# One pair more of the first MLP products in VectorE's written order

## The chip, the cores and the metric

The kernel runs on one core of one Trainium2 chip. Its time is the device time of one launch in microseconds (us); three runs of the kernel before gave 1718.39, 1720.16 and 1721.22 us, and the median, 1720.16, is the time before. Engines are called PE (TensorE), DVE (VectorE), ACT (ScalarE), POOL (GpSimd) and SP (SyncE, which issues most of the DMAs here).

## The reference

Two sequences of 512 tokens with 1024 features go through a trunk of two layers in float32: a Fourier token mixer and an MLP, then grouped-query attention and an MLP, each behind an RMS norm and with a residual, and a last RMS norm. The change lies in the MLPs alone:

```python
def sq_relu_mlp(h, w_up, w_down):
    a = jnp.maximum(h @ w_up, 0)
    return (a * a) @ w_down
...
        x = x + sq_relu_mlp(rms_norm(x, mlp_norm[i]), mlp_w_up[i], mlp_w_down[i])
```

with `w_up` of 1024 x 4096 and `w_down` of 4096 x 1024, the same weights for both sequences.

## The kernel before

**Numbers and products.** Every float32 matrix is split into two float32r halves: ACT casts it to the high half (line 82) and DVE subtracts that from the original to get the low half (line 83). A product of two split matrices is three matmuls per block. The MLP's first product, `h @ w_up`, is done by a 2x2 scheme with seven block products in place of eight (as Strassen and Winograd do it). The two sequences are the two columns of the scheme, the two halves of the features its inner index, and two neighbouring blocks of 128 hidden units its rows. Such two blocks are a pair. Layer 0 has 16 pairs; layer 1 has 14 and four hidden blocks done plainly.

**One pair.** A pair p takes seven products of 12 matmuls each (4 feature blocks x 3 matmuls of 128 x 512, line 833). `Pair.first` and `Pair.second` multiply the row of raw weights (a11, a12) with the operands b11 and b21; they fill the PSUM bank `self.o`. `Pair.rest` does the other five, with sums of weight blocks as the left factor: s2 into bank ob, s3 into oc, s1 into od, then a22 added on to oc and s4 added on to od. Behind each of them DVE adds a finished bank to something kept: line 911 (the first addition, ob + t gives u2), line 915 (the second, oc + u2 gives u3), line 924 (the third, od + u3), line 933 (oc + u2, after a22's product) and line 942 (od + u2, after s4's product). The matmuls that add on to oc or od may start only when line 915 or line 924 has read that bank. ACT then squares the results (lines 848, 849), POOL takes four differences of them (lines 950 to 953), and ACT's and SP's DMA queues write seven results to memory (line 843; those issued by SP are the spills called t1 to t4).

**What is prepared meanwhile.** While pair p is multiplied, DVE and ACT prepare pair p + 1: its sums of weight blocks (`sums_13`, lines 882 and 883, and `sum_2`, line 886, and `sum_4`, line 894) and the splits of these and of its row. `split_row` splits the row of raw weights, 128 x 1024, for `first` and `second`; `split_23` splits s2 and s3 together, `split_1` splits s1 and a22, `split_4` splits s4. The raw weights of pair p + 2 are loaded by SP (line 91) into a pool of five buffers, which hold two loads and one tile of sums for each pair.

**Order.** The tables `AHEADS = (8, 6)` say for how many pairs of each layer `first` and `second` are done ahead, in a first sweep over the pairs (the value is `ah` in the code). For these pairs only the five products of `rest` are left in the second sweep; the row of pair `ah` and of every later one is split, and its two products done, in the second sweep (such a pair is `late`). The framework's scheduler sets the order of each engine's instructions from the order of the program and its own planning; inside `tc.manual_schedule(engines={ET.DVE})` DVE's instructions stay in the order in which the code writes them. In the second sweep that holds for the pairs p < ah; later pairs are left to the scheduler. Each engine works off its list strictly in order, and so does SP with its DMA issues.

Of the kernel before, what the change touches and what calls it, by code (L numbers as in the profile page):

```python
# [40 lines left out]
def trunk_kernel(ctx, tc, x_in, xt_in, y_out, dcos, dsin, feat, rope, gfour, gcol, grow, gfin,  # L41
# [22 lines left out]
    def tm(shape=(P, 512), dt=F32):  # L64
        return tmp.tile(list(shape), dt, tag="t2", name=nm("t"))
# [4 lines left out]
    def ps():  # L70
        return psp.tile([P, 512], F32, tag="ps", name=nm("ps"))
# [569 lines left out]
    ET = mybir.EngineType  # L641
# [185 lines left out]
    def product(o, w, h, first=True):  # L827

        n = len(h)
        for k in range(n):  # L830
            sl = slice(k * P, (k + 1) * P)
            for i, (x, y) in enumerate(((0, 0), (0, 1), (1, 0))):
                nc.tensor.matmul(o, w[x][:, sl], h[k][y], start=first and k + i == 0,  # L833
                                 stop=k == n - 1 and i == 2, skip_group_check=not first)

    def first_product(l, blocks, rows, ahead):
        def b(name):
            return [(h[0][:, i], h[1][:, i]) for h in blocks.b[name] for i in range(2)]
# [6 lines left out]
        np_, ah = NPS[l], AHEADS[l]  # L845

        def squares(t, src):
            nc.scalar.activation(t, src, AF.Relu)
            nc.scalar.activation(t, t, AF.Square)  # L849

        class Pair:
# [55 lines left out]
            def rest(self, nxt, fill=iter(())):  # L907
                ob, oc, od = ps(), ps(), ps()
                u2, u3, t = tm(), tm(), self.t
                product(ob, self.s2, b("t2"))  # L910
                nc.vector.tensor_add(u2, ob, t[:, 0])  # L911
                if nxt:
                    nxt.sums_13()
                product(oc, self.s3, b("t3"))
                nc.vector.tensor_add(u3, oc, u2)
                if self.late:
                    self.second()
                if nxt:
                    nxt.sum_2()
                if nxt and self.late:  # L920
                    nxt.split_row()
                next(fill, None)
                product(od, self.s1, b("t1"))
                nc.vector.tensor_add(u3, od, u3)  # L924
                if nxt and nxt.p == ah:
                    nxt.split_row()
                squares(u3, u3)
                if nxt:
                    nxt.split_23()
                product(oc, self.a22, b("t4"), False)  # L930
                next(fill, None)
                v = tm()
                nc.vector.tensor_add(v, oc, u2)
                squares(v, v)
                if nxt:
                    nxt.sum_4()
                    nxt.split_1()
                next(fill, None)
                if nxt:
                    nxt.split_4()  # L940
                product(od, self.s4, b("b22"), False)
                nc.vector.tensor_add(t[:, 0], od, u2)
                squares(t[:, 0], t[:, 0])
                return t[:, 1], t[:, 0], v, u3
# [91 lines left out]
        def early(ahead):  # L1036

            pairs[-1].first()
            pairs[-1].second()
            pairs[-1].late = False  # L1040
            for _ in range(3):
                yield next(ahead)

        for p, pair in enumerate(pairs[:-1]):
            if p >= ah:
                pair.first()
            with tc.manual_schedule(engines={ET.DVE}) if p < ah else nullcontext():
                done = pair.rest(pairs[p + 1], early(ahead) if not last and p == np_ - 2 else iter(()))
            if p + 2 < len(pairs):
                if p + 2 >= ah:  # L1050
                    pairs[p + 2].load()
                pairs[p + 2].load_sums()
            elif last:
                last[0].load()
            if not last and p == np_ - 3:
                next(ahead)
            pair.out(*done, queue=nc.sync if last or p < np_ - 2 else nc.gpsimd)
# [12 lines left out]
    def second_product(l, blocks, rows, late=lambda: None, ready=lambda m: None):  # L1070
# [179 lines left out]
        def finish(m):  # L1250
            left[m] -= 1
            if left[m] == 0:
                nc.vector.tensor_add(xs[0, m][:, 1], xs[0, m][:, 1], e[m])
                nc.vector.tensor_add(xs[1, m], xs[1, m], e[m].unsqueeze(1).broadcast_to([P, 2, 512]))
                ready(m)

        first_product(l, blocks, rows, ahead)
        e += [tm() for _ in range(4)]
        items, waiting = [], []
# [296 lines left out]
    for n in range(1, len(heads) + 1):  # L1556
        pts, nxt = [], []
# [309 lines left out]
```

## Time and profile before

| | us |
|---|---|
| time of the three runs, median | 1720.16 |
| time of the profiled execution | 1717.6 |
| its span, first to last instruction | 1715.8 |
| PE busy in the span | 1691.0 |
| DVE busy | 1239.0 |
| ACT busy | 857.8 |
| POOL busy | 335.5 |

Rows of the timeline give the start, the duration, the engine, the line, the operation, output and input tiles, how many instructions were merged into the row and, in brackets, how long the engine had stood idle before it and whose work ended that idle time. Matmuls overlap, so that a row of twelve lasts a little longer than the distance from its start to the next row's start; distances between starts give the pace. Letters ahead of an arrow name what is written, those behind it what is read: ps is a PSUM bank, w and u are tiles of halves or results, t a smaller temporary, raw a tile of raw weights or of their sums.

In layer 0 the second sweep's pair 8 (`ah`) begins with PE at 257.9 us, in layer 1 pair 6 at 1213.5 us.

### The profile page before, as it was taken

To read this page: it belongs to the slowest core of one execution; us is meant where nothing else is said; L and a number is where in the kernel's file an instruction comes from. 1 tells how busy PE (TensorE), PEld (TensorE's weight loads), DVE (VectorE), ACT (ScalarE), POOL (GpSimd) and SP (SyncE) were. 2 spreads that over 40 slices of the span, in tenths; PEclk is the share of its full clock that TensorE was granted. 3 is DMA by queue.
4 is the path that set the end of the run, shared out by engine and by line. 5 is a ranking of instruction groups with operands and counts; after the bars stand their busy time and mean duration, and the time that the engine had idled before them with its cause. 6 is when DMAs were issued, how large, how long until landed. Compare 5 with 4: busy or idle time off the path is not lost. (4 is left out here: it accounts for less than half of the span.)

```text
span 1715.8 us, 21892 instructions
## 1 busy us (share of the span) xinstructions
PE 1691.0 (99%) x7847; PEld 1395.8 (81%) x7847; DVE 1239.0 (72%) x1836; ACT 857.8 (50%) x1508; POOL 335.5 (20%) x302
## 2 busy tenths in 40 slices
PE   9999999999999999999999999999999999999997
PEld 6988887888788888888877888788788888888886
DVE  8679776456887879976588834687655479787865
ACT  6666445446343434457687714554444544344334
POOL 1321442321000000232244303114422200000004
PEclk9999999999999999999999999999999999999999
DMA  9742554449554645610000213335534686455322
GB/s 322 191 143 95 196 202 163 161 172 367 197 197 138 214 148 175 232 42 28 26 25 1 99 50 123 110 114 197 181 142 148 225 303 237 163 204 193 115 74 99
DMA packets 103679, 266.33 MB, mean 155 GB/s; under 512 B 10177, under 2 KB 10177, under 8 KB 103570
## 3 DMA queue, kind: packets, MB, share of 16 engines
q1 hardware_dynamic: 87410, 232.95, 38.4%
q10 hardware_dynamic: 14112, 25.70, 4.0%
q0 software_dynamic: 2048, 6.29, 1.8%
q8 instruction: 61, 1.00, 0.2%
q14 instruction: 48, 0.39, 0.1%
HBM read 189.93 MB, written 73.92 MB: 154 GB/s over the span
## 5 line engine op out<-in xcount | busy, mean ns | idle before, releaser
L833 PE MATMUL ps<-u,w 128*128 128x512 f32 x4656 | 1068.9, 390 | 5.3 <-DVE w L83 1.2
L833 PEld LDWEIGHTS ps<-u,w 128*128 128x128 f32 x4656 | 873.4, 188 | 192.3 <-DVE w L83 2.7
L82 ACT CAST w<-raw 128x1024 fp32r<-128x1024 f32 (+1 forms) x224 | 217.6, 981 | 435.8 <-PE ps L833 266.6
L83 DVE TENSOR_TENSOR w<-raw,w 128x1024 fp32r<-128x1024 f32 (+1 forms) x224 | 258.0, 1154 | 71.9 <-ACT w L82 71.5
L159 POOL TENSOR_TENSOR t<-t,t 128x512 f32<-128x512 f32 (+1 forms) x56 | 79.0, 1410 | 738.1 <-ACT t L157 682.0
L83 DVE TENSOR_TENSOR u<-u,u 128x1024 fp32r<-128x1024 f32 x132 | 157.6, 1220 | 25.8 <-ACT u L82 25.2
L82 ACT CAST u<-u 128x1024 fp32r<-128x1024 f32 x132 | 132.4, 1044 | 70.5 <-PE ps L833 48.5
L77 PE MATMUL ps<-u,u 128*128 128x512 f32 (+2 forms) x388 | 150.0, 388 | 1.9 <-DVE u L496 1.4
L1089 DVE TENSOR_TENSOR u<-ps,u 128x512 f32<-128x512 f32 x160 | 109.4, 686 | 53.9 <-PE ps L833 53.3
L78 PE MATMUL ps<-u,u 128*128 128x512 f32 (+2 forms) x388 | 144.8, 373 | 1.4 <-DVE u L83 1.4
L79 PE MATMUL ps<-u,u 128*128 128x512 f32 (+2 forms) x388 | 144.5, 372 | 0.0
L833 PE MATMUL ps<-u,u 128*128 128x512 f32 x576 | 138.2, 391 | 2.4 <-DVE t L924 2.3
L833 PEld LDWEIGHTS ps<-u,u 128*128 128x128 f32 x576 | 107.6, 188 | 27.1 <-DVE t L924 2.6
L950 POOL TENSOR_TENSOR u<-u 128x512 f32<-128x512 f32 x28 | 36.6, 1305 | 411.3 <-ACT u L849 411.3
L83 DVE TENSOR_TENSOR u<-ps,u 128x512 fp32r<-128x512 f32 (+4 forms) x118 | 74.6, 650 | 17.4 <-ACT u L82 16.2
L78 PEld LDWEIGHTS ps<-u,u 128*128 128x128 f32 x388 | 73.4, 189 | 14.1 <-DVE u L83 3.9
L77 PEld LDWEIGHTS ps<-u,u 128*128 128x128 f32 x388 | 73.5, 190 | 13.8 <-DVE u L496 1.6
L79 PEld LDWEIGHTS ps<-u,u 128*128 128x128 f32 x388 | 73.1, 188 | 13.0 <-DVE u L83 0.4
L911 DVE TENSOR_TENSOR t<-ps,u 128x512 f32<-128x512 f32 x30 | 20.7, 690 | 81.8 <-PE ps L833 63.8
L82 ACT CAST u<-ps 128x512 fp32r<-128x512 f32 (+4 forms) x118 | 64.6, 562 | 28.8 <-PE ps L79 10.9
L816 DVE TENSOR_TENSOR u<-ps,u 128x512 f32<-128x512 f32 (+1 forms) x48 | 30.8, 644 | 64.8 <-PE ps L79 64.8
L77 PE MATMUL ps<-u,w 128*128 128x512 f32 (+2 forms) x192 | 64.9, 338 | 0.0
(237 smaller groups left out, 2005.8 us busy)
## 6 DMA issues: line engine op xcount, KB each, us to landing
raw<-w_up SPq DMA_DIRECT2D x82, 512.0 KB, 4.5
u<-spill_t SPq DMA_DIRECT2D x60, 512.0 KB, 6.1
raw<-w_sum SPq DMA_DIRECT2D x56, 512.0 KB, 4.0
u<-spill_b SPq DMA_DIRECT2D x45, 512.0 KB, 5.2
spill_t<-u SPq DMA_DIRECT2D x87, 256.0 KB, 2.0
spill_b<-t ACTq DMA_DIRECT2D x60, 256.0 KB, 3.2
raw<-w_row SPq DMA_DIRECT2D x28, 512.0 KB, 4.1
park<-u SPq DMA_DIRECT2D x24, 512.0 KB, 3.3
```

The costliest lines, as they stand in the source:

```text
L77: nc.tensor.matmul(out, lh, rh, start=first, stop=False)
L78: nc.tensor.matmul(out, lh, rl, start=False, stop=False)
L79: nc.tensor.matmul(out, ll, rh, start=False, stop=last)
L82: nc.scalar.copy(dst_hi, src)
L83: eng.tensor_sub(dst_lo, src, f32(dst_hi))
L159: nc.gpsimd.tensor_add(acc[q][:, :n], acc[q][:, :n], s[:, :n])
L816: nc.vector.tensor_add(x[:, :n], o[:, :n], x[:, :n])
L833: nc.tensor.matmul(o, w[x][:, sl], h[k][y], start=first and k + i == 0, stop=k == n - 1 and i == 2, skip_group_check=not first)
L911: nc.vector.tensor_add(u2, ob, t[:, 0])
L950: eng.tensor_sub(t[:, 0], b12, b11)
L1089: nc.vector.tensor_add(x, o, x)
```

## The change

The written order of DVE holds for p <= ah, that is for one pair more in each layer: pair 8 in layer 0 and pair 6 in layer 1. Within the code of that pair, the call that splits the next pair's row is moved from ahead of the third product (s1) to behind the third addition, line 924, where pair ah - 1 already had it. Pairs after `ah` keep it where it was. Products, tiles and instructions are the same in number and kind.

```diff
@@ -917,12 +917,12 @@
                     self.second()
                 if nxt:
                     nxt.sum_2()
-                if nxt and self.late:
+                if nxt and self.p > ah:
                     nxt.split_row()
                 next(fill, None)
                 product(od, self.s1, b("t1"))
                 nc.vector.tensor_add(u3, od, u3)
-                if nxt and nxt.p == ah:
+                if nxt and ah - 1 <= self.p <= ah:
                     nxt.split_row()
                 squares(u3, u3)
                 if nxt:
@@ -1044,7 +1044,7 @@
         for p, pair in enumerate(pairs[:-1]):
             if p >= ah:
                 pair.first()
-            with tc.manual_schedule(engines={ET.DVE}) if p < ah else nullcontext():
+            with tc.manual_schedule(engines={ET.DVE}) if p <= ah else nullcontext():
                 done = pair.rest(pairs[p + 1], early(ahead) if not last and p == np_ - 2 else iter(()))
             if p + 2 < len(pairs):
                 if p + 2 >= ah:
```

PE, ACT and POOL keep their rows one for one in both layers. Two lists change, in the same way in each layer; the rows are shown for layer 0.

VectorE's list from the end of pair 7 on, before. Tiles of pair 8's results are ps_2543 to ps_2545, u_2528 and t_2546 to t_2547; raw_2511 and raw_2513 are pair 9's raw weights, raw_2561 its sums, w_2592 its split row, w_2610 its s2 and s3, w_2631 its s1 and a22; raw_2652, raw_2654 and raw_2702 belong to pair 10:

```order
L882 TENSOR_TENSOR raw_2561<-raw_2511,raw_2513 128x512
L83 TENSOR_TENSOR w_2592<-raw_2511,w_2592 128x1024
L883 TENSOR_TENSOR raw_2513<-raw_2513 128x512
L886 TENSOR_TENSOR raw_2561<-raw_2513,raw_2511 128x512
L83 TENSOR_TENSOR w_2610<-raw_2561,w_2610 128x1024
L911 TENSOR_TENSOR t_2546<-ps_2543,u_2528 128x512
L915 TENSOR_TENSOR t_2547<-ps_2544,t_2546 128x512
L83 TENSOR_TENSOR w_2631<-raw_2513,w_2631 128x1024
L882 TENSOR_TENSOR raw_2702<-raw_2652,raw_2654 128x512
L883 TENSOR_TENSOR raw_2654<-raw_2654 128x512
L886 TENSOR_TENSOR raw_2702<-raw_2654,raw_2652 128x512
L924 TENSOR_TENSOR t_2547<-ps_2545,t_2547 128x512
```

The same place now. The tiles have new numbers: pair 8's banks are ps_2545 to ps_2547, its sums t_2548 and t_2549, pair 9's sums raw_2563, its row w_2607, its other halves w_2612 and w_2633:

```order
L911 TENSOR_TENSOR t_2548<-ps_2545,u_2528 128x512
L882 TENSOR_TENSOR raw_2563<-raw_2511,raw_2513 128x512
L883 TENSOR_TENSOR raw_2513<-raw_2513 128x512
L915 TENSOR_TENSOR t_2549<-ps_2546,t_2548 128x512
L886 TENSOR_TENSOR raw_2563<-raw_2513,raw_2511 128x512
L924 TENSOR_TENSOR t_2549<-ps_2547,t_2549 128x512
L83 TENSOR_TENSOR w_2607<-raw_2511,w_2607 128x1024
L83 TENSOR_TENSOR w_2612<-raw_2563,w_2612 128x1024
L933 TENSOR_TENSOR t_2627<-ps_2546,t_2548 128x512
L894 TENSOR_TENSOR t_2631<-raw_2511,raw_2563 128x512
L83 TENSOR_TENSOR w_2633<-raw_2513,w_2633 128x1024
```

The three additions of pair 8 (lines 911, 915, 924) have moved ahead: two of pair 9's three sums stand between the first and the second addition, the third sum between the second and the third, and the subtractions of the splits behind the third. Pair 10's sums have left this stretch; they, with the subtraction of its row's split, now follow line 942 of pair 8, ahead of pair 9's line 911.

SP's list at the same place before (spill_t_1 are pair 7's results, raw_2793 is pair 11's):

```order
L91 DMA raw_2511<-w_up 128x1024
L91 DMA raw_2513<-w_up 128x1024
L91 DMA raw_2652<-w_up 128x1024
L91 DMA raw_2654<-w_up 128x1024
L843 DMA spill_t_1_1228<-u_2515 128x512
L843 DMA spill_t_1_1232<-u_2515 128x512
L843 DMA spill_t_1_1236<-u_1565 128x512
L843 DMA spill_t_1_1240<-t_2516 128x512
L91 DMA raw_2793<-w_up 128x1024
```

and now (raw_2655 and raw_2657 are pair 10's, raw_2796 is pair 11's):

```order
L91 DMA raw_2511<-w_up 128x1024
L91 DMA raw_2513<-w_up 128x1024
L843 DMA spill_t_1_1228<-u_2515 128x512
L843 DMA spill_t_1_1232<-u_2515 128x512
L843 DMA spill_t_1_1236<-u_1565 128x512
L843 DMA spill_t_1_1240<-t_2516 128x512
L91 DMA raw_2655<-w_up 128x1024
L91 DMA raw_2657<-w_up 128x1024
L91 DMA raw_2796<-w_up 128x1024
```

Pair 10's two loads have moved behind pair 7's four spills, and stand together with pair 11's.

## The prediction

> **What bounds the kernel now.** I read the page first, then the waits of PE, then PE's timeline around the pairs that the diff names, then DVE's, ACT's, SP's and POOL's at the same microseconds, and last the chain of waits.
>
> ```profile
> PE 1691.0 (99%) x7847; PEld 1395.8 (81%) x7847; DVE 1239.0 (72%) x1836; ACT 857.8 (50%) x1508; POOL 335.5 (20%) x302
> ```
>
> PE is the bound: only its pauses can be won. The view of PE's waits (us in total, times, the longest) names these two among its largest:
>
> ```profile
> PE ps L833 <- DVE t L924: 2.3, 3, 0.9
> PE ps L833 <- DVE t L915: 1.1, 2, 0.7
> ```
>
> Those are the waits of a product that adds on to a bank which DVE has not read yet. The timeline of PE, layer 0, pair 8 (its ob begins at 260.58) and pair 9 (from 278.89):
>
> ```profile
> 260.58 5.60 PE L833 MATMUL ps<-u,w 128*128 128x512 f32 x24
> 266.02 2.88 PE L833 MATMUL ps<-u,u 128*128 128x512 f32 x12
> 268.75 2.88 PE L833 MATMUL ps<-u,w 128*128 128x512 f32 x12
> 272.09 3.01 PE L833 MATMUL ps<-u,w 128*128 128x512 f32 x12 [0.46 <-DVE t L915]
> 276.00 3.06 PE L833 MATMUL ps<-u,u 128*128 128x512 f32 x12 [0.90 <-DVE t L924]
> 278.89 16.48 PE L833 MATMUL ps<-u,w 128*128 128x512 f32 x72
> 295.21 2.88 PE L833 MATMUL ps<-u,u 128*128 128x512 f32 x12
> ```
>
> The rows are, in turn, ob and oc; the row's second product; od; a22; s4; then six products of pair 9 in one piece and its s4. And layer 1, pair 6 and pair 7:
>
> ```profile
> 1216.18 5.60 PE L833 MATMUL ps<-u,w 128*128 128x512 f32 x24
> ...
> 1227.89 3.02 PE L833 MATMUL ps<-u,w 128*128 128x512 f32 x12 [0.67 <-DVE t L915]
> 1231.80 3.06 PE L833 MATMUL ps<-u,u 128*128 128x512 f32 x12 [0.90 <-DVE t L924]
> 1234.70 16.48 PE L833 MATMUL ps<-u,w 128*128 128x512 f32 x72
> 1251.02 2.88 PE L833 MATMUL ps<-u,u 128*128 128x512 f32 x12
> ```
>
> So four of the five waits on lines 915 and 924 sit in the two pairs that the change touches. Why DVE is late there stands in its timeline of pair 8:
>
> ```profile
> 261.83 0.68 DVE L882 TENSOR_TENSOR raw<-raw,raw 128x512 f32<-128x512 f32 x1
> 262.43 1.22 DVE L83 TENSOR_TENSOR w<-raw,w 128x1024 fp32r<-128x1024 f32 x1
> 263.57 1.78 DVE L883 TENSOR_TENSOR raw<-raw 128x512 f32<-128x512 f32 x1
> 265.38 1.67 DVE L886 TENSOR_TENSOR raw<-raw,raw 128x512 f32<-128x512 f32 x1
> 268.16 2.38 DVE L83 TENSOR_TENSOR w<-raw,w 128x1024 fp32r<-128x1024 f32 x1 [1.12 <-ACT w L82]
> 270.46 0.68 DVE L911 TENSOR_TENSOR t<-ps,u 128x512 f32<-128x512 f32 x1
> 271.34 0.69 DVE L915 TENSOR_TENSOR t<-ps,t 128x512 f32<-128x512 f32 x1 [0.20 <-DVE t L911]
> 271.95 1.21 DVE L83 TENSOR_TENSOR w<-raw,w 128x1024 fp32r<-128x1024 f32 x1
> 273.20 0.69 DVE L882 TENSOR_TENSOR raw<-raw,raw 128x512 f32<-128x512 f32 x1
> ...
> 275.26 0.68 DVE L924 TENSOR_TENSOR t<-ps,t 128x512 f32<-128x512 f32 x1
> ```
>
> Bank ob is full at 260.58 + 2.72 = 263.3, yet line 911 runs at 270.46: three sums and two subtractions for pair 9 stand ahead of it, one of them waiting for an ACT cast. Line 924, whose bank is full at about 271.6, stands behind pair 10's three sums and runs at 275.26. The end of the chain of waits (start, us, what) tells what a microsecond of this is worth:
>
> ```profile
> 1231.80 160.82 PE ps L833 x708
> 1392.64 264.82 PE ps L833 x1164
> ```
>
> From the stall at 1231.80 on the chain is PE's own work until 1657 us.
>
> **The change, part by part.** The numbers are layer 0's; layer 1 has the same rows 955.6 us later.
>
> *The two waits.* The distance of 72 matmuls without a pause is 295.21 - 278.89 = 16.32 us, 2.72 a product (1251.02 - 1234.70 gives 16.32 too). The 72 from pair 8's ob to pair 9's first take 278.89 - 260.58 = 18.31, in layer 1 1234.70 - 1216.18 = 18.52. The pauses therefore cost 1.99 and 2.20, together 4.19 us. Of this 0.46 + 0.90 + 0.67 + 0.90 = 2.93 is named as idle; the rest is the slower restart (3.01 to 3.06 for twelve where 2.88 is usual) and the ends of the products. These are the two bounds of the gain, 2.93 and 4.19; I take 4.19, since starts are what moves the end. More cannot come: PE then has no pause left here.
>
> *Does the new order reach the banks in time?* Rows from ACT and from DVE's pair 7, which has the new order already:
>
> ```profile
> 263.15 0.57 ACT L867 COPY u<-ps 128x512 f32<-128x512 f32 x1
> 252.62 0.69 DVE L924 TENSOR_TENSOR t<-ps,t 128x512 f32<-128x512 f32 x1 [0.60 <-PE ps L833]
> 257.41 1.05 ACT L82 CAST w<-raw 128x1024 fp32r<-128x1024 f32 x1 [2.76 <-DMA raw<-w_up]
> ```
>
> Line 911 needs the copy that ends at 263.72. Then 0.68 for it, 0.68 and 1.78 for lines 882 and 883: line 915 runs at 266.9 to 267.6. The product a22 is due at 268.75 + 2.72 = 271.47, 3.9 later. Line 886 (1.67) ends at 269.3. Line 924 then waits for PE, as pair 7's did, until od ends at about 271.6, and is done at 272.4; s4 is due at 274.19, 1.8 later. Both waits go.
>
> *What becomes later.* The subtraction of pair 9's row follows line 924: 1.22, done at 273.6. The cast that it needs ran at 257.41. Pair 9's first product is due at 260.58 + 16.32 = 276.90, so 3.3 are left; the cover is pair 8's s4, and without it every microsecond would be PE's. Its s2 and s3 (1.22) are done at 274.8, due at 279.62. Its s1 and a22 follow line 933, that is 274.3 + 0.69 + 0.68 + 1.22 = 276.9, due at 287.78. Cost on PE: nothing.
>
> *SP's queue.* Pair 10's two loads now stand behind four spills that wait for POOL:
>
> ```profile
> 253.64 4.64 SPq L91 DMA_DIRECT2D raw<-w_up  x4
> 269.49 0.32 SPq L843 DMA_DIRECT2D spill_t<-t  x1
> raw<-w_up SPq DMA_DIRECT2D x82, 512.0 KB, 4.5
> 277.79 1.05 ACT L82 CAST w<-raw 128x1024 fp32r<-128x1024 f32 x1 [0.45 <-ACT t L849]
> 280.61 0.69 DVE L942 TENSOR_TENSOR u<-ps,t 128x512 f32<-128x512 f32 x1
> ```
>
> All four loads were issued by 258.3; pair 10's will be issued at about 269.9 and land, by the page's median of 4.5, at 274.4. ACT's cast of pair 10's row, which ran at 277.79, can run at 274.4. Queued behind it on ACT are the squares of line 933's result and the cast of pair 9's s4, and on DVE behind that cast the s4 subtraction, line 942, and then pair 10's sums and pair 9's line 911. I follow the last: from the cast to the end of line 942 is 280.61 + 0.69 - 277.79 = 3.51; lines 882, 83, 883 and 886 take, as at 261.83 to 267.05, 5.22; from there to the end of the subtraction at 271.95 are 6.12 (two split subtractions, the additions, the cast); line 924 takes 0.69. Sum 15.54. It must be over by 276.90 + 16.32 = 293.22, so the cast may start as late as 277.68: the loads may take 7.8 us in place of 4.5. Bounds: nothing up to 7.8, one for one beyond. I take nothing, as 4.5 is far nearer. Pair 11's loads are due for the same moment as before.
>
> *Contention of DVE and POOL.* The four rows at 261.83 lie beside POOL's work on pair 7; the same operation without POOL is faster:
>
> ```profile
> 263.33 1.47 POOL L950 TENSOR_TENSOR u<-u 128x512 f32<-128x512 f32 x1 [10.14 <-ACT u L849]
> 294.02 0.69 DVE L883 TENSOR_TENSOR raw<-raw 128x512 f32<-128x512 f32 x1
> ```
>
> Line 883 takes 1.78 beside POOL, 0.69 alone. Pair 10's sums ran without POOL and now stand behind line 942, where POOL begins on pair 8; the 5.22 above is that slow price already, and it costs nothing while the 3.3 us of margin hold.
>
> [...]
>
> *Sum.* 1717.6 - 4.19 = 1713.4 for the profiled execution. It lay 1.8 above its span of 1715.8 and 2.6 below the median; off the median, 1720.16 - 4.19 = 1716.0.
>
> **The rivals.** *Layer 0's gain is lost in the second product.* Between the MLP's two products DMA is full, and PE waits there soon after:
>
> ```profile
> 388.00:442.00 54.00, 53.47 (x236) 43.83 (x235) 38.16 (x44) 35.72 (x45) 7.26 (x8) 1.00 1.02 388
> 453.11 17.11 PE L833 MATMUL ps<-u,w 128*128 128x512 f32 x74 [1.00 <-DVE w L83]
> ```
>
> The last three columns of the first row are granted clock, DMA's busy share and GB/s. If the loads, not PE, set the moment 453.11, then arriving 1.99 earlier only lengthens the wait, and 2.20 remain: 1718.0. Against it: the loads of that stretch are issued as PE, DVE and POOL free buffers, so they come earlier too.
>
> *The wait comes back one pair later.* Pair 10's sums now stand ahead of pair 9's line 911, just as pair 9's stood ahead of pair 8's. [...] If the whole old stall returns, 4.19 are lost again, 1720.2. For it: the same pattern of rows. Against it: `second` lies between oc and od of pair 9 as well, and pair 9's list has one split fewer ahead of line 911.
>
> *Slower: pair 10's loads come too late.* The place is SP's queue, the price one for one from 7.8 us of landing. In the full stretch loads do take that long:
>
> ```profile
> u<-spill_b SPq DMA_DIRECT2D x8, 512.0 KB, 9.6
> ```
>
> At 9.6 the stall is 1.8 a layer, and 0.6 of the gain is left. From 7.8 + 4.19 / 2 = 9.9 on the change loses, and at 12, which also delays pair 11's loads, 2 x 4.2 - 4.19 = 4.2: 1724.4. For it: one queue in strict order, and all the lead that these loads had, 12 us, is gone. Against it: DMA is not full there, and loads just ahead took 3.8 (253.64 to the cast at 257.41).
>
> **How the numbers follow.** A measurement of this kernel tells about 0.2%, 3.4 us, from no change. The forecast, both waits gone and nothing in their place: chance 0.68, at 1716.0, its own range 1714.5 to 1717.4 (gain of 2.93 to 4.19, with the scatter of the runs, 1718.39 to 1721.22). Of it 0.58 count as faster and 0.10 as the same, as 4.19 stands only 0.75 above the bound. Layer 0's gain lost: 0.14, same. The wait comes back: 0.08, same. Loads too late: 0.10, of which 0.09 slower. That makes faster 0.58, same 0.33, slower 0.09. The predicted time is 1716.0. The range 1714.0 to 1719.6 holds nearly all of the forecast, the first rival, part of the second and the mildest form of the third.
>
> **What would show it.** Right: no bracket with L915 or L924 on PE in pair 8 and pair 6, pair 9's first 16.32 after pair 8's ob, line 911 about 0.5 after ob ends, pair 10's cast at about 274 to 276, and the granted clock as before. Wrong: a pause of PE in pair 9 or pair 7 of layer 1 (second and third rival; the bracket at the ACT cast would name the load), or a longer wait near 451 (first rival).

## The result and the profile after

| | kernel before | changed kernel | ratio, 95% interval |
|---|---|---|---|
| first comparison, 16 runs each | 1718.78 us | 1715.48 us | 0.9979 (0.9971 to 0.9987) |
| second, 21 and 11 runs | 1719.03 us | 1714.15 us | 0.9976 (0.9967 to 0.9985) |
| third, 11 and 5 runs | 1720.28 us | 1715.15 us | 0.9969 (0.9956 to 0.9981) |

The medians fell by 3.3, 4.9 and 5.1 us. Forecast were 4.19 us, a ratio of 0.9976, which lies in all three intervals, and 1716.0 for the time. The profiled execution took 1716.4 us, with a span of 1714.6. Its granted clock (the share of PE's full clock that the profile shows as allowed) was 0.997 on average, as before. PE's busy time is the same to a tenth:

```profile
PE 1691.0 (99%) x7847; PEld 1397.4 (81%) x7847; DVE 1238.6 (72%) x1836; ACT 858.3 (50%) x1508; POOL 338.5 (20%) x302
```

Of PE's waits on the additions (us in total, times, the longest) one is left, which belongs to another pair (near 410 us, there before too), and none on line 915. Line 1089 (DVE's additions in the MLP's second product) made PE wait once before, 0.93 us near 715 us; now it does so twice, 1.24 there and 0.79 near 1405 us:

```profile
PE ps L833 <- DVE u L1089: 2.0, 2, 1.2
...
PE ps L833 <- DVE t L924: 0.5, 1, 0.5
```

The timeline of PE, pair 8 of layer 0 (ob begins at 262.06) and pair 9 (from 278.38), then pair 6 of layer 1 and the start of pair 7:

```profile
262.06 5.60 PE L833 MATMUL ps<-u,w 128*128 128x512 f32 x24
267.50 2.88 PE L833 MATMUL ps<-u,u 128*128 128x512 f32 x12
270.22 5.60 PE L833 MATMUL ps<-u,w 128*128 128x512 f32 x24
275.66 2.88 PE L833 MATMUL ps<-u,u 128*128 128x512 f32 x12
278.38 16.48 PE L833 MATMUL ps<-u,w 128*128 128x512 f32 x72
294.70 2.88 PE L833 MATMUL ps<-u,u 128*128 128x512 f32 x12
...
1216.22 5.60 PE L833 MATMUL ps<-u,w 128*128 128x512 f32 x24
...
1232.55 16.48 PE L833 MATMUL ps<-u,w 128*128 128x512 f32 x72
```

No row has a bracket. The 72 matmuls of pair 8 take 278.38 - 262.06 = 16.32 us, 1.99 less than before, and pair 9's take 16.32 again. In layer 1, pair 6's 72 matmuls take 1232.55 - 1216.22 = 16.33, which is 2.2 less. DVE in pair 8:

```profile
265.15 0.69 DVE L911 TENSOR_TENSOR t<-ps,u 128x512 f32<-128x512 f32 x1 [1.90 <-ACT u L867]
265.75 0.73 DVE L882 TENSOR_TENSOR raw<-raw,raw 128x512 f32<-128x512 f32 x1
266.52 1.66 DVE L883 TENSOR_TENSOR raw<-raw 128x512 f32<-128x512 f32 x1
268.11 0.68 DVE L915 TENSOR_TENSOR t<-ps,t 128x512 f32<-128x512 f32 x1
268.71 1.18 DVE L886 TENSOR_TENSOR raw<-raw,raw 128x512 f32<-128x512 f32 x1
273.14 0.69 DVE L924 TENSOR_TENSOR t<-ps,t 128x512 f32<-128x512 f32 x1 [3.25 <-PE ps L833]
```

Line 911 runs 265.15 - (262.06 + 2.72) = 0.37 us after its bank is full, in place of 7.2. Line 924 now waits for PE, where PE waited for it. The chain of waits has no stop in pair 6 any more, and a new one behind 1400 us:

```profile
1096.18 291.58 PE ps L833 x1284
...
1405.46 250.75 PE ps L833 x1104
```

**Why the two profiled spans differ by only 1.2 us.** Granted clock is the third column from the right in these stretches, first of the changed kernel, then of the one before:

```profile
78.60:82.00 3.40, 3.40 (x18) 3.40 (x17) 1.34 (x6) 2.04 (x5) 0.00 (x0) 0.50 0.00 0
...
112.80:116.20 3.40, 3.40 (x10) 2.64 (x9) 2.67 (x7) 0.62 (x3) 0.00 (x0) 0.51 0.01 2
```

```profile
78.60:82.00 3.40, 3.40 (x30) 3.30 (x29) 1.46 (x7) 3.14 (x6) 0.00 (x0) 1.00 0.00 0
...
110.80:114.20 3.40, 3.37 (x9) 2.64 (x9) 2.67 (x8) 1.16 (x4) 0.00 (x0) 0.50 0.01 2
```

Ahead of 1700 us the execution of the changed kernel had two stretches of 3.4 us at half clock, that of before one. Up to 78 us both start the same matmuls at the same moment; behind 82 us the changed kernel is 1.45 late, 150 us ahead of the first changed instruction. From there its starts gain 1.98 in pair 8 and 2.20 in pair 6, lose 0.56 between 715 and 1182 us, 0.31 of it at once in the wait on line 1089 near 715 us, and lose 0.86 near 1405 us: 1.47 - 1.98 + 0.56 - 2.20 + 0.86 = -1.29 at 1407 us, and -1.24 at the end. That wait near 715 us varies between executions of one kernel: it is 0.93 us in this profile of the kernel before and 1.2 in its second one, and 1.24 and 1.4 in the first two of the changed kernel. Whether the earlier arrival has a part in it stays open.

### The profile page after: what moved, and what is told of

Read it like the earlier page. It is cut to its first block, busy times and chain, and to the rows that moved or that the text cites. A ratio compares the mean times of both kernels' runs of the same rounds, so it can differ in the third digit from the quotient of the medians.

```text
span 1714.6 us, 21900 instructions
## 1 busy us (share of the span) xinstructions
PE 1691.0 (99%) x7847; PEld 1397.4 (81%) x7847; DVE 1238.6 (72%) x1836; ACT 858.3 (50%) x1508; POOL 338.5 (20%) x302
```

## The experiments

**One layer alone.** The pair more is written out in layer 0 only, or in layer 1 only (`l != 1` in place of `l != 0`):

```diff
-                if nxt and self.p > ah:
+                if nxt and self.p > ah - (l != 0):
...
-                if nxt and ah - 1 <= self.p <= ah:
+                if nxt and ah - 1 <= self.p <= ah - (l != 0):
...
-            with tc.manual_schedule(engines={ET.DVE}) if p <= ah else nullcontext():
+            with tc.manual_schedule(engines={ET.DVE}) if p <= ah - (l != 0) else nullcontext():
```

> Only layer 0's pair 8 is changed; layer 1 is as before. If the gain is the two waits on lines 915 and 924 alone, the 72 matmuls from pair 8's ob on take 16.32 us in place of 18.31, layer 1's stay at 18.52, and the time falls by about 2.0 us (0.12%). If the second product takes layer 0's gain back (the first rival), PE's distance to the kernel before is back at nothing by 455 us and the time does not move.

> Only layer 1's pair 6 is changed. The 72 matmuls from its ob on take 16.32 in place of 18.52. If the pause of 0.8 us near 1405 us in the changed kernel comes from PE arriving 2.1 us earlier while a load does not land 2.1 earlier, it shows here too, and the time falls by about 1.4 us (0.08%). If that pause was an accident of one execution it does not show, and the time falls by 2.1 (0.13%).

Measured: 1717.17 (ratio 0.9988, 0.9978 to 0.9998) and 1717.75 (0.9986, 0.9978 to 0.9995), both beside 1719.04. Each layer gives its own part: 1.2 and 1.4 thousandths, together 2.6 where the whole change gave 2.1, 2.4 and 3.1; each of these figures is uncertain by about one thousandth. The pauses of the layer that stayed are still there. With the change in layer 0 alone, PE's timeline of layer 1 shows

```profile
1226.39 3.02 PE L833 MATMUL ps<-u,w 128*128 128x512 f32 x12 [0.55 <-DVE t L915]
1230.30 3.02 PE L833 MATMUL ps<-u,u 128*128 128x512 f32 x12 [0.89 <-DVE t L924]
```

and its 72 matmuls take 18.36 us. In the changed kernel layer 0's gain of 1.98 still stood whole up to 710 us, behind the DMA-full stretch, so that stretch does not take it back.

**The order without the split's place.** The written order holds for p <= ah, but the split stays ahead of the third product:

```diff
-                if nxt and self.p > ah:
+                if nxt and self.late:
...
-                if nxt and ah - 1 <= self.p <= ah:
+                if nxt and nxt.p == ah:
```

> The written order holds for one pair more, but the next row's split stays ahead of the third product, so that its subtraction (1.22 us) stands ahead of line 924 on VectorE and nothing else differs from the changed kernel. If the order does the work and the place of the split none: the subtraction fits into the 3 us that VectorE waits ahead of line 924, no pause of PE, time as the changed kernel (about 3.5 us under the kernel before). If the split's place matters: line 924 later by up to 1.2 and a pause of PE ahead of s4, up to 0.7 a layer given back.

Measured: 1715.56, ratio 0.9978 (0.9969 to 0.9987). DVE's timeline of its pair 8:

```profile
270.34 2.31 DVE L83 TENSOR_TENSOR w<-raw,w 128x1024 fp32r<-128x1024 f32 x1
273.33 0.69 DVE L924 TENSOR_TENSOR t<-ps,t 128x512 f32<-128x512 f32 x1 [0.68 <-PE ps L833]
```

The row's subtraction stands ahead of line 924 and takes 2.31, yet line 924 still waits 0.68 for PE. PE has no pause there, as in the changed kernel. So the written order alone makes the gain, and the split's new place adds nothing that the comparison (good to about 1.5 us) or PE's timeline shows. The converse, the split moved with the order left to the scheduler, was not run: every engine's list of instructions is then the list of before.

**Two pairs more.** The same three conditions with `ah + 1` in place of `ah`:

> The written order holds for two pairs more (p <= ah + 1), with the split behind the third addition there too. Pair 9 (pair 7 in layer 1) had no pause of PE before nor after the change. If only PE's pauses count: the same time as the changed kernel within 0.1%. If DVE's order there has a worth of its own, or the loads that now stand behind one more set of spills come too late: a pause of PE in that pair or the next, slower by its length.

Measured: 1716.5, ratio 0.9978 (0.9969 to 0.9987). Pair 9's line 911 now runs when its bank is full, but no PE pause was left there to win.

**The kernel before and the changed one, a second profile each.**

> The kernel before once more, for a second profile. The change loses 0.8 us of its 4.19 behind 1400 us, where PE pauses 0.79 for line 1089 (the second product of layer 1 waits for the sums of w_down); the first profile of before shows no pause there. Theory A (the pause is scatter of the loads between executions): this profile may show a pause of 0.3 to 0.9 for line 1089 between 1404 and 1411 although nothing is changed. Theory B (the pause is the earlier arrival, 2.1 us, at loads whose landing does not move: the first rival, in layer 1): no pause there, as in the first profile. The two waits on lines 915 and 924 in pairs 8 and 6 stand as before under both, with 18.3 and 18.5 us for their 72 matmuls. I also expect one to three stretches of 3.4 us at half granted clock before 120 us, at other places than in the first profile.

> The change once more, on one chip with the kernel with four writes. Times 1715.5 again, ratio to before 0.998 (4.19 us less the 0.8 us lost near 1405 is 3.4 of 1719). In the profile: no bracket for lines 915 and 924 in pairs 8 and 6, 16.32 us for their 72 matmuls, and the pause near 1405 for line 1089 again (0.5 to 0.9) if it belongs to the changed program, absent if it is scatter.

The spans are 1719.7 and 1716.0. By luck both executions have their half-clock stretches at nearly the same places, three each (36.5, 80.8 and 115.0 before; 36.2, 80.6 and 114.7 with the change), so these two can be set against each other. The changed kernel's starts are 0.24 ahead at the first product of pair 8, 2.36 ahead behind it, 4.56 ahead behind pair 6 of layer 1, and 3.66 ahead at the end. What is given back lies near 1405 us (0.24) and, for the most part, at 1435 us:

```profile
1434.75 5.53 PE L833 MATMUL ps<-u,w 128*128 128x512 f32 x23 [0.50 <-DVE w L83]
```

The pause of 0.79 near 1405 us is not in this profile. Its cause in the first one is a load of sums of w_down. The timelines of SP, DVE and PE there:

```profile
1394.32 3.68 SPq L91 DMA_DIRECT2D raw<-w_sum  x3
...
1401.45 0.42 DVE L1156 TENSOR_TENSOR raw<-raw,raw 128x256 f32<-128x256 f32 x1 [2.61 <-DMA raw<-w_sum]
...
1405.46 3.05 PE L833 MATMUL ps<-u,u 128*128 128x512 f32 x12 [0.79 <-DVE u L1089]
```

and in the second profile of the changed kernel:

```profile
1396.38 3.60 SPq L91 DMA_DIRECT2D raw<-w_sum  x3
...
1402.26 0.42 DVE L1156 TENSOR_TENSOR raw<-raw,raw 128x256 f32<-128x256 f32 x1 [1.44 <-DMA raw<-w_sum]
```

From issue to use the load took 7.1 us in one execution and 5.9 in the other, of the same program. The pause stands in six profiles (0.79, with one layer alone 0.51 and 0.74, order alone 0.95, two pairs more 0.48, and 0.26 in a third profile of the changed kernel) and is absent in both profiles of before, in one of the changed kernel and in the three with spare writes below. (In the two with the sums' loads first, below, these loads have another order.) It is thus not fixed by the program. That the earlier arrival makes it more frequent is likely by this count, but not shown; it cost at most 0.95 us.

**Pair 10's loads made later: four, eight and twelve spare writes.** To price the third rival, one result tile is written four, eight or twelve times more to a spare tensor, by SP, behind pair ah - 1's last spill and ahead of the loads in question, in each layer:

```diff
-        np_, ah = NPS[l], AHEADS[l]
+        np_, ah = NPS[l], AHEADS[l]; spare = drm.tile([8, P, 512], F32, name=f"spare_{l}")
...
-                    put(op, p, x, queue)
+                    put(op, p, x, queue); op == "t4" and p == ah - 1 and [queue.dma_start(spare[i], x) for i in range(8)]
```

> As the kernels with eight and twelve spare writes, with four in each layer. With eight, the loads were issued 6.78 us later and the cast of pair 10's row ran 6.76 later (276.88 to 283.64), so four put it at about 280.3. New theory, from the rows of the kernel with eight: PE resumes 5.26 us after the cast, behind ACT's copy L867, and is due there 8.16 after pair 9's first product, so the cast may be as late as 278.4 + 8.16 - 5.26 = 281.3, and line 924, 13.74 behind the cast, allows 281.0: no pause in pair 9 or in layer 1's pair 7, 1715.5 like the changed kernel (ratio to before 0.998). The recorded working (deadline 279.2 in this frame, one for one beyond): a pause of 1.1 in each layer, about 1717.7. On the pause of 0.5 to 0.9 near 1405 (line 1089), which five profiles of kernels that gain show and four of kernels that don't gain lack: if it comes with the earlier arrival it is here too; if it comes with the place of the tensors in memory, which the spare tensor moves, it is absent as with eight and twelve.

> The change, plus eight further writes of one result tile (256 KB each) to a spare tensor in each layer, on SP right behind pair ah - 1's last spill, so that pair ah + 2's loads are issued behind them. The third rival's price: from the changed kernel's rows the cast of pair 10's row may be 2.3 us later than it was before PE has to wait. With eight writes the loads land some 5.5 us later (a load of the same size takes about 0.7 us of the DMA at full rate). Theory (margin, then one for one): PE pauses about 3.2 us in pair 9 of layer 0 and, as layer 1's cast waited for PE and not for the load, 2 to 3 in pair 7 of layer 1: 1715.5 + 5 to 6.5 = 1720.5 to 1722. Rival (the loads have more cover than I worked out, or the writes pass through DMA beside the loads): no pause, 1715.5. Rival (the writes also delay pair 11's loads and the wait is met twice): 1725 or more.

> As the kernel with eight spare writes, with twelve in each layer, so that the loads land about 2.8 us later again (8.3 us later than in the changed kernel). Theory (margin, then one for one): each layer loses 2.8 us more than with eight, 5.5 us in all: about 1726 to 1727.5. If the margin is larger than I worked out, twelve cost less, but what they cost over eight still goes one for one as soon as eight cost anything. Rival (not one for one, DMA takes the loads beside the writes): under 1718.

Measured beside the kernel before: 1714.36 with four (ratio 0.9977, 0.9969 to 0.9986), 1720.47 with eight (1.0008, 0.9999 to 1.0018) and 1725.42 with twelve (1.0035, 1.0023 to 1.0048). With eight, PE in pair 9 of layer 0 and then in layer 1's pair 7 shows a pause in each:

```profile
278.41 8.32 PE L833 MATMUL ps<-u,w 128*128 128x512 f32 x36
288.90 10.07 PE L833 MATMUL ps<-u,w 128*128 128x512 f32 x36 [2.17 <-ACT u L867]
...
1236.37 8.32 PE L833 MATMUL ps<-u,w 128*128 128x512 f32 x36
1246.51 8.45 PE L833 MATMUL ps<-u,w 128*128 128x512 f32 x36 [1.81 <-ACT u L867]
1255.06 3.04 PE L833 MATMUL ps<-u,u 128*128 128x512 f32 x12
```

and ACT and DVE beside pair 9:

```profile
283.64 1.05 ACT L82 CAST w<-raw 128x1024 fp32r<-128x1024 f32 x1 [5.95 <-DMA raw<-w_up]
...
288.29 0.57 ACT L867 COPY u<-ps 128x512 f32<-128x512 f32 x1
```

```profile
286.97 0.68 DVE L882 TENSOR_TENSOR raw<-raw,raw 128x512 f32<-128x512 f32 x1
...
292.08 0.68 DVE L911 TENSOR_TENSOR t<-ps,u 128x512 f32<-128x512 f32 x1
...
296.70 0.68 DVE L924 TENSOR_TENSOR t<-ps,t 128x512 f32<-128x512 f32 x1
```

The eight writes delayed the loads by 6.8 us, where 5.5 were expected (eight times 256 KB take 5.4 us at the 388 GB/s that DMA moved from 388 to 442 us in the kernel before): SP took 6.58 us to issue them. The late cast (after 5.95 of waiting for the load) holds up ACT's copy L867, and the copy holds up PE, a stop that the prediction did not have. From the cast to the end of line 924 are 297.38 - 283.64 = 13.74 us. Line 924 is due 16.32 after the pair's first product, so by this the cast may come up to 16.32 - 13.74 = 2.58 after that product, and each microsecond beyond costs one. The 13.74 are from layer 0 with eight writes; three other places test the rule. With four writes the cast of layer 1 comes 2.19 after the product (1238.29 and 1236.10) and the 72 matmuls take 16.32, so it costs nothing, while layer 0's comes 3.02 after it. PE and ACT in layer 0:

```profile
280.31 16.75 PE L833 MATMUL ps<-u,w 128*128 128x512 f32 x72
297.14 3.02 PE L833 MATMUL ps<-u,u 128*128 128x512 f32 x12
```

```profile
283.33 1.05 ACT L82 CAST w<-raw 128x1024 fp32r<-128x1024 f32 x1 [6.18 <-DMA raw<-w_up]
```

The 72 take 297.14 - 280.31 = 16.83, 0.51 more, where the rule says 3.02 - 2.58 = 0.44. With eight, layer 1's cast comes 4.87 after the product:

```profile
1241.24 1.05 ACT L82 CAST w<-raw 128x1024 fp32r<-128x1024 f32 x1 [6.70 <-DMA raw<-w_up]
```

The rule says 2.29, and the 72 take 1255.06 - 1236.37 = 18.69, 2.37 more. Layer 0's comes 5.23 after it: the rule says 2.65 and the pause costs 288.90 - 278.41 - 8.16 = 2.33 (8.16 is 36 matmuls at full pace); the rest is hidden by what follows it, a stretch at half clock (below) that costs 1.75 by itself. Between the two places with a clean price the cast moves by 1.85 and the cost by 1.86. So the price is one for one, as predicted, but it begins later. The recorded working had a pause in both layers with four writes, and the newer theory had none; there was one, of 0.51, in layer 0 alone.

With twelve the price does not follow the rule, and this run says less than it should. The scheduler here puts the row's cast behind that of s4's split on ACT, so that line 942 no longer waits for the load, and the profile shows 4.65 us lost in layer 0, a stretch at half clock included, where the rule says 5.7 (the cast came 8.3 after the product), and 3.94 in layer 1. These 8.6 us and the changed kernel's median of 1715.5 make 1724.1; the median is 1725.42. Set against the changed kernel's profiled execution (1716.4) they make 1725.0, and this profiled execution took 1725.49. What makes the rest, 0.5 to 1.3, stays open.

**The sums' loads first.** The loads of the sums of w_down are issued ahead of the residual's in each chunk of the second products:

```diff
+                self.x, self.y = sums_raw(self.m, self.g, self.n)
...
-                self.x, self.y = sums_raw(self.m, self.g, self.n)
```

> The change, with the loads of the sums of w_down issued ahead of the residual's loads in each chunk of the second products of both layers (the scheduler moves some DVE and ACT instructions with them). In the changed kernel PE pauses 0.8 near 1405 us behind such a load of sums (DVE L1156 waits for raw<-w_sum), and 0.5 near 410 and 1.0 near 453 in layer 0. If these pauses are set by the moment at which the sums' loads are issued, 0.8 to 1.8 us go: 1713.7 to 1714.7. If DMA is full there and only the order among the loads changes, some other tile becomes the late one and the time is the same or worse: 1715.5 to 1718.

> The change with the loads of the sums of w_down ahead of the residual's, once more, on one chip with the changed kernel. It gave 1713.8, but its profile had no stretch at half clock before 1700 us, and its pauses after pair 6 add up to 0.6 us as in the changed kernel. Theory: no different from the changed kernel run beside it, the medians within 1 us. Rival: the earlier loads take away 0.8 us or more, the median 1 to 2 us below the changed kernel's.

> The change beside the kernel with the sums' loads first. 3.3 to 4.9 us below the kernel before, as in the two comparisons so far (ratio 0.997 to 0.9985).

Measured: 1713.82 at first (ratio 0.9969, 0.9957 to 0.998), then 1715.22 (0.9973, 0.9961 to 0.9984) beside the changed kernel's 1715.15 (0.9969, 0.9956 to 0.9981) on one chip. No difference. The low first value goes with the clock: four of its six executions had a granted clock of 0.998, where the median of the kernel before beside them was 0.997. The one profiled ran at full clock from 12 to 1700 us, and its 0.998 is the highest granted clock of the profiled executions here (the others have 0.995 to 0.997):

```profile
12.00:1700.00 1688.00, 1676.16 (x7815) 1388.07 (x7814) 1226.86 (x1795) 847.02 (x1486) 334.24 (x293) 1.00 0.45 155
```

## Why the prediction was right

- *The two waits go, 4.19 us.* Right, with its size: 72 matmuls take 16.32 in both layers, 1.99 and 2.20 less. Three comparisons gave 3.3, 4.9 and 5.1 us, each good to 1.4 to 2.2 us. The prediction held 3.4 us for the least that one measurement tells from no change: the first fall lies just under it, the others above. The upper bound, read from starts, was the right one to take; the named idle time (2.93) would have missed the slower restart. That 1716.0 came within 0.5 of the measured 1715.48 is in part luck: it was counted from a median of three runs, 1720.16, and sixteen runs of the same kernel gave 1718.78. From there the forecast would have been 1714.6.
- *The new order reaches the banks in time.* Right: line 911 at 0.37 after its bank is full (forecast 0.5); line 915 ends at 268.79, 4.1 ahead of its product (forecast 3.9), and line 924 waits for PE.
- *The split's new place.* The prediction costed pair 9's row at nothing, with 3.3 us left. With the split in its old place the time is the same, so this half of the change is neutral. The prediction had not separated the two halves.
- *SP's queue.* Nothing lost, as taken, but two sizes were off and partly cancelled. The loads landed in 276.88 - 271.49 = 5.4 us, not 4.5. SP and ACT in the changed kernel:

```profile
271.49 7.30 SPq L91 DMA_DIRECT2D raw<-w_up  x4
```

```profile
276.88 1.06 ACT L82 CAST w<-raw 128x1024 fp32r<-128x1024 f32 x1 [1.66 <-DMA raw<-w_up]
```

  And the sum of 15.54 from the cast to the end of line 924 is 13.74. Its terms 3.51 and 5.22 measured 3.33 and 5.11; the one mis-sized is the last, 6.12 + 0.69 = 6.81 against 297.38 - 292.08 = 5.30. It had been taken from a stretch of before in which DVE waited 1.12 for a cast and one subtraction took 2.38. The cast may come 2.58 after the pair's first product, not 0.78. As the cast ran 1.50 ahead of that product, the margin is 4.1 us, in place of 3.3.
- *Contention of DVE and POOL.* Right in that it costs nothing: in the changed kernel pair 10's four operations stand where forecast, line 883 at the slow price (1.77 beside POOL's line 950, which runs from 281.71 for 1.47), and line 915 behind them waits for PE:

```profile
281.95 1.77 DVE L883 TENSOR_TENSOR raw<-raw 128x512 f32<-128x512 f32 x1
...
286.80 0.69 DVE L915 TENSOR_TENSOR t<-ps,t 128x512 f32<-128x512 f32 x1 [0.77 <-PE ps L833]
```

- *First rival, layer 0's gain lost in the second product.* Refuted where it was put: the DMA share from 388 to 442 us is 1.03, the wait near 452 is 1.00 as before, and the gain passes. Something like it happens in small in layer 1, where a late load of sums takes back up to 0.95 us in some executions.
- *Second rival, the wait returns one pair later.* Refuted: pair 9 and pair 7 take 16.32, and one pair more in the written order brings nothing. No run shows a return of part of the wait, which the range counts in: pair 10's four operations took 285.42 - 280.22 = 5.20 us in the changed kernel, the last three of them beside POOL, where the working had 5.22.
- *Third rival, pair 10's loads too late.* Its mechanism is real and its price one for one, but in layer 0 the change stays 4.1 us away from it. Eight writes, which put the cast 6.8 us later, are needed to use up the gain.

## What to carry to other kernels

When a strict queue lets a consumer's work wait behind preparation for the next item, put the operations that free a bank first, and fill the gap behind them; check each moved load by the time from its landing to the next point at which the bound engine must wait, along every engine that stands in between. Read the price of a stall from the distance between starts, not from the idle time named in brackets. And before two profiles are compared for a change of a few microseconds, line up the starts of the same instruction ahead of the change: what differs there is not the change.

## What the runs showed of the hardware

**Stretches at half clock in the middle of a busy kernel.** Stretches of the second profile of the changed kernel (PE's busy time stands behind the comma; granted clock is third from the right), three at half clock and the one ahead of the first:

```profile
32.80:36.20 3.40, 1.85 (x14) 1.44 (x13) 3.04 (x5) 3.40 (x7) 0.31 (x1) 1.00 1.05 234
36.20:39.60 3.40, 3.40 (x17) 3.40 (x18) 3.37 (x4) 3.16 (x4) 0.87 (x1) 0.51 1.05 276
...
80.60:84.00 3.40, 3.40 (x18) 3.40 (x18) 1.18 (x5) 2.47 (x5) 0.00 (x0) 0.50 0.00 0
...
114.70:118.10 3.40, 3.40 (x9) 2.62 (x8) 2.39 (x7) 0.30 (x3) 0.00 (x0) 0.51 0.01 2
```

Each lasts 3.4 us, and they lie 44.4 and 34.1 us apart, 13 and 10 times 3.41. In the first profile of the changed kernel half clock begins at 78.62 and 112.75 us and, behind PE's last matmul, at 1710.19: 34.13 and 1597.44 apart, 10 and 468 times 3.413. In the first of before it begins at 110.76 and 1708.19, again 468 times 3.413 apart. In each of these three the places fall on one such grid, and it lies differently in each execution: 78.62 and 110.76 are 9.4 steps apart. Ahead of each of the three rows above at half clock PE was not fully busy: 1.85 of 3.40 us ahead of the first, 2.62 and 2.58 ahead of the others. PE's instructions ahead of 120 us are the same in all kernels here, and their profiles show none to three of these stretches there. The number differs with where the grid lies: the two executions with a stretch at 36.2 and at 36.5 us have three each, at nearly the same places, the one with its first at 78.6 has two, the one with its first at 110.8 one. The one at 78.6 us cost 1.45 us. That is a good part of the scatter between runs of one kernel: over the 33 runs of the kernel before beside the one-layer kernels, time falls by 1.2 us for each 0.001 of granted clock (correlation -0.75), and one stretch takes 3.41 x 0.5 of 1716 us, 0.001. A new pause can bring one too. With eight spare writes:

```profile
286.70:290.10 3.40, 1.23 (x6) 1.02 (x6) 3.40 (x4) 1.73 (x3) 1.56 (x2) 1.00 0.25 93
290.10:293.50 3.40, 3.40 (x9) 2.67 (x9) 3.16 (x4) 1.15 (x2) 3.40 (x3) 0.51 0.41 154
```

```profile
1242.40:1245.80 3.40, 2.29 (x11) 1.56 (x9) 2.44 (x4) 2.54 (x5) 0.00 (x0) 1.00 0.66 261
1245.80:1249.20 3.40, 2.69 (x12) 2.24 (x13) 3.37 (x3) 0.66 (x2) 3.06 (x3) 1.00 0.20 77
```

Layer 0's pause of 2.17 us fell into one stretch of the grid, which left PE busy for 1.23 of 3.40, and the next ran at half clock: 9 matmuls in place of the 16 or 17 of a full one. Layer 1's pause of 1.81 fell across a border (1245.80, which is 280 steps of 3.413 behind 290.10; 2.29 and 2.69 busy), and the clock stayed at 1.00. So of two pauses of some 2 us one cost itself and 1.75 more, the other itself alone. How much work keeps the clock is not settled by the busy time that the profile shows: with eight writes the stretch of the grid at 1242.4 us was busy for 2.29 of 3.40 with 11 matmuls and kept it, while the one busy for 2.62 ahead of 80.6 us, with 23 smaller matmuls, did not.
